# Transformer encoder block in float32 on one core: fixed queue places for the tile and pair operations of the mixed MLP part, spread norm rows, other banks in the last half

## The chip, the cores and the metric

The kernel runs on one core of a Trainium2 chip. The metric is device time in microseconds of one execution, the median of several. Five engines work on their own instruction queues: TensorE (PE, whose weight loads are shown as PEld), VectorE (DVE), ScalarE (ACT), GpSimd (POOL) and SyncE (SP), which here issues the loads and stores. [...]

## What is computed

One layer on 256 tokens of width 2048, all in float32:

```python
x <- LN1(alpha*x + W_out [GQA-group(x) ; MLA-group(x)])   # combined input projection
x <- LN2(alpha*x + CrossAttn(x, LNm(mem)))                # 4 heads, 256 memory tokens
x <- LN3(alpha*x + W2 relu(W1 x)^2)                       # squared-ReLU MLP, width 8192

def squared_relu_mlp(h, w_mlp_in, w_mlp_out):
    return jnp.square(jax.nn.relu(h @ w_mlp_in)) @ w_mlp_out
```

The change lies in the last line, the MLP, which takes the last 60% of the time.

## The kernel before

**Splits.** A float32 product is made of three matmuls on numbers of a shorter format. Each weight piece `raw` (128x1024 float32) is split in two: ACT writes `w_hi` (line 955), then DVE writes `lo = raw - w_hi` (line 956). There are four buffers for `w_hi` and four for `lo`, so a split can be made at most four splits ahead of the matmuls that use it. `mm3` (lines 164 to 166) issues the three matmuls hi*hi, lo*hi, hi*lo. In the list of items below the splits of a pass can be counted 1, 2, 3 and so on; the change counts in them.

**Items.** The hidden layer of the MLP has 64 tiles of 128 columns (4 chunks `c` of `CH` = 16). The first eight are made by `hidden_group`, in two groups of four. After that the order of work is a list `items` of two kinds, and a loop `one_pass(c, q)` goes through it in eight passes (four chunks, two halves `q` of the output columns):

- A hidden tile `("g", c, j)` (`hidden_tile`): two splits, 16 matmuls with `w_hi` (line 1020) and 16 with `lo` (line 1028) into one bank of PSUM `ps`.
- A unit `("u", c, q, p)` multiplies two hidden tiles with their rows of W2. The first six units of a pass (`SEVEN`) use a scheme of seven products in place of eight: 4 splits, of which the last two take sums of weights `s_t`, which DVE makes in three additions (line 948). Units 6 and 7 are plain, with two splits. The last pass has plain units alone.

In passes with q = 1 the list reads g u g u and so on: g has splits 1 and 2, u has 3 to 6, g has 7 and 8, u 9 to 12. In passes with q = 0 it is the same but for one place where two hidden tiles follow each other. Seven passes hold hidden tiles.

**Tile and pair operations.** When a hidden tile is done, `evacuate` brings it out of PSUM: ACT copies one half (line 870) and DVE adds the other (line 871), into one half of a `tmp` tile `h`. When the second of a pair (odd `j`) is there, `stages` follows: `square` is relu and square on ACT (lines 883, 884); `halve` splits the result into `ht`, on ACT (line 874) and DVE (line 875); `add` makes four sums of it on DVE (lines 894, 897, 898); `halve_sums` splits these into `aux` (lines 874, 875 again).

**Pass ends.** After the sixth unit `banks` gets eight additions on DVE that bring the products out of PSUM into `res` (lines 1092, 1094, 1097); at the end of a pass four `merge` calls bring the sums x22, x12, x11, x21 out. `norm_ops(1)` are four multiplications and additions of 128x1024 with the rows of LN2 (line 1194); they must precede the merges of the pass (0, 1).

**What sets the order.** A scheduler places instructions. `queue(ins)` binds an instruction behind the last one queued on its engine, so queued ones keep the order of the code; an instruction under `free_order` is placed by the scheduler. Before, the splits and matmuls are queued, and so are sums and norm rows, which hang at splits through `side`, `banks` and `sums`. The evacuations, most of `stages` (called later, through `late_finish`) and the merges are free.

**Loads.** SP loads each item's 1 MB (line 935) into one of four buffers in turn, and from the item `JOIN` on into one of five: `row_b`, which held the norm rows, joins them.

Of the kernel before, what the change touches and what calls it, by code (L numbers as in the profile page):

```python
# [33 lines left out]
CH = 16  # L34
# [4 lines left out]
def encoder_kernel(ctx: ExitStack, tc: tile.TileContext, t, out):  # L39
# [869 lines left out]
    for c, q in PASSES:  # L909
# [3 lines left out]
        for u in us:  # L913
            n = 2 if q == 0 and u[3] == (CH // 2 - 2 if c else 0) else 1
            items += gs[:n] + [u]
            gs = gs[n:]
    JOIN = items.index(("u", 1, 0, 0))

    def fetch():

# [37 lines left out]
    def part(src, hi=None, lo=None):  # L958
        w = src.shape[1]
        if hi is None:  # L960
            hi = wsp.tile([P, 1024], F32R, tag="w_hi", name="w_hi")
        if lo is None:
            lo = lo_tile()
        queued_split(hi[:, :w], lo[:, :w], src)
        if banks:
            pump()
        if sums:
            sums.popleft()()
        else:
            pump()  # L970
        return hi[:, :w], lo[:, :w]
# [35 lines left out]
    def both(*todo):  # L1007
        return [lambda: [x() for x in todo]]

    now, late_finish = [], []  # L1010

    def hidden_tile(it, ps):

        _, c, j = it
        for h_ in range(2):
            hi, lo = part(raw_of[it][:, h_ * 1024:(h_ + 1) * 1024])
            k0 = 8 * h_

            def w_hi(k):
                queue(nc.tensor.matmul(ps, hi[:, k * P:(k + 1) * P], x2t[:, k0 + k, :],  # L1020
                                       start=k0 + k == 0, stop=k0 + k == KT - 1))

            for k in range(7):
                w_hi(k)
            if h_ == 0:
                w_hi(7)
            for k in range(8):
                queue(nc.tensor.matmul(ps[:, 0:S], lo[:, k * P:(k + 1) * P], x2t[:, k0 + k, 0:S],  # L1028
                                       start=False, stop=False))
            if h_ == 1:  # L1030
                w_hi(7)
        if j % 2 == 0:
            now[:] = [tmp_tile()]
        evacuate(ps, now[0], j % 2)
        if j % 2:
            def rest(h=now[0]):
                for stage in stages(h, c, j // 2, queue if j == CH - 1 else free_order):
                    stage()
            if (c, j) == (0, LEAD + 1):
                x1, x2, x3, x4 = stages(now[0], c, j // 2, queue)  # L1040
                side.extend([x1] + both(x3, x2) + [x4])
            else:
                late_finish.append(rest)

    bank = []
    at = [0]

    def step():

        it = items[at[0]]  # L1050
        at[0] += 1
        if it[0] == "g" and late_finish:
            late_finish.pop()()
        fetch()
        if at[0] < len(items) and not is_seven(it) and is_seven(items[at[0]]):
            push_sums(items[at[0]])
        return it
# [9 lines left out]
    def one_pass(c, q):  # L1067
# [2 lines left out]
        final = (c, q) == PASSES[-1]  # L1070
        if final:
            wide = big.tile([P, 8192], F32R, tag="big", name="wide")
        (x11, x12, x21, x22), (p1, p5, p6, p7) = xs, pt = bank[:4], bank[4:]
        left = {id(ps): len(sevens) * (ps is not x22) + 2 * (len(order) - len(sevens)) for ps in xs}
        left.update({id(ps): len(sevens) for ps in pt})
        left[id(x22)] -= 2 * HELD * final
# [12 lines left out]
        def merge(r, x, op=ALU.add):  # L1089
            if any(r is y for y in fresh):  # L1090
                fresh[:] = [y for y in fresh if y is not r]
                nc.vector.scalar_tensor_tensor(out=r, in0=r, scalar=ALPHA, in1=x, op0=ALU.mult, op1=op)
            else:
                nc.vector.tensor_tensor(out=r, in0=r, in1=x, op=op)  # L1094

        def more(ps, op=ALU.add):
            nc.vector.tensor_tensor(out=m_t, in0=m_t, in1=ps, op=op)
# [2 lines left out]
        while n_unit < len(order):  # L1100
            it = step()
            if it[0] == "g":
                if n_unit == 0:
                    ps = {LEAD: x22, LEAD + 1: x21}[it[2]] if it[1] == 0 else p6
                elif n_seven < len(sevens):
                    ps = x22
                else:
                    spare = spare or [p1, p6]
                    ps = spare[0]
                    spare.reverse()  # L1110
                hidden_tile(it, ps)
                continue
            p, raw, k = it[3], raw_of[it], 2 * it[3]
            n_unit += 1
            if p in sevens:
                if n_seven == 0:
                    while banks:
                        banks.popleft()()
                while sums:
                    sums.popleft()()  # L1120
                for src, todo in ((raw[:, 512:1536], ((p1, a(c, k, 0)), (x12, sm(c, p, 3)))),
                                  (raw[:, 1536:2048], ((x11, a(c, k + 1, 0)),)),
                                  (s_t[:, 0:1024], ((p5, sm(c, p, 1)), (p7, sm(c, p, 0)))),
                                  (s_t[:, 1024:2048], ((p6, sm(c, p, 2)), (x21, a(c, k + 1, 1))))):
                    for (hi, lo), (ps, x) in zip(halves(part(src)), todo):
                        mm(ps, x, hi, lo)
                n_seven += 1
                if at[0] < len(items) and is_seven(items[at[0]]):
                    push_sums(items[at[0]])
                if n_seven == len(sevens):  # L1130
                    nc.scalar.activation(m_t, p1, AF.Copy)

                    rows0, rows1 = late_rows[(c, q)] if (c, q) in late_rows else ([], [])
                    banks.extend(rows0 + [lambda: merge(r11, m_t), lambda: more(p6),
                                  lambda: merge(r12, m_t, ALU.subtract), lambda: more(p7, ALU.subtract)] + rows1 + [
                                  lambda: merge(r21, m_t), lambda: merge(r22, m_t, ALU.subtract),
                                  lambda: merge(r22, p5), lambda: merge(r12, p5)])
            elif final and len(order) - n_unit < HELD:
                n = len(parts) // 2
                for i in range(2):  # L1140
                    o = (2 * n + i) * 1024
                    lo = sums_h[2 * n + i - 1] if n + i else lo_tile()
                    w = halves(part(raw[:, i * 1024:(i + 1) * 1024], wide[:, o:o + 1024], lo))
                    parts.append((k + i, w))
                    for (hi, lo), ps in zip(w, (x12, x11)):
                        mm(ps, a(c, k + i, 0), hi, lo)
            else:
                for i in range(2):
                    w = halves(part(raw[:, i * 1024:(i + 1) * 1024]))
                    for (hi, lo), to in zip(w, ((x12, x22), (x11, x21))):  # L1150
                        for b in range(2):
                            mm(to[b], a(c, k + i, b), hi, lo)
            if q == 1:
                give("h", c, p)
                if p in SEVEN:
                    give("s", c, p)
            if late_finish:
                late_finish.pop()()
        if not final:
            for r, ps in ((r22, x22), (r12, x12), (r11, x11), (r21, x21)):  # L1160
                merge(r, ps)
            if c == NCH - 1:
                banks.extend([lambda b=b, r=r: stats(sts[b], r)
                              for b, r in ((0, r11), (0, r12), (1, r21), (1, r22))])
            return
        pump(len(banks))
        merge(r22, x22)

        def done(b, r, ps):
# [28 lines left out]
    for g in range(LEAD // G):  # L1198
        empty, (first, second) = hidden_group((lambda k: w_mi0[k // 2]) if g == 0 else (lambda k: s_in.next()),
                     att_tile if g % 2 else acc_tile, 0, g * G, first_pair if g == 0 else None)  # L1200
        wait = [lambda: None]

        if g == 0:
            norm_rows(0)
            rows = norm_ops(0)
            (a1, a2, a3, a4), (b1, b2, b3, b4) = first, second
            side.extend(wait * 4 + empty + [a1, b1, a3, a2, a4, b3] + both(b2, rows[0])
                        + both(b4, rows[1]) + rows[2:])
            s_in.split, s_in.beside = queued_split, 2
        else:  # L1210
            (a1, a2, a3, a4), (b1, b2, b3, b4) = first, second
            assert not side
            side.extend(wait + both(*empty) + [a1] + both(a3, a2) + [a4, b1] + both(b3, b2) + [b4])
            norm_rows(1)
    bank[:] = [acc_tile() for _ in range(4)] + [att_tile() for _ in range(4)]
    n1 = norm_ops(1)
    late_rows = {(0, 1): (n1[0::2], n1[1::2])}
    for cq in PASSES:
        one_pass(*cq)

    g3, b3 = s_t, raw_of[items[-5]]
# [137 lines left out]
```

## Time and profile before

| what | value |
| --- | --- |
| runs, us | 1104.68, 1105.43, 1540.56; median 1105.43 |
| profiled execution, us | 1104.5 (span 1102.7, 1.8 us lie around it) |
| mean granted TensorE clock | 0.995 |
| PE busy in the span | 1080.1 us, 98% |
| DVE busy | 936.3 us, 85% |
| ACT busy | 638.4 us, 58% |
| DMA engines, mean share | about 55% |

The profile gives one execution on the chip. A matmul's shown length is longer than the distance to the next one, since matmuls overlap: those of 512 columns are shown with 389 ns and start 227 ns apart. So PE counts as busy through short waits, and a wait is best read from the distance of two starts. DVE and ACT instructions overlap by some 80 ns as well: what one costs in a row of its kind is the distance of starts, 1.135 us for a split of 1024 columns shown with 1.22 us.

The mixed part of the MLP (hidden tiles and units) runs from 447 us to 1046 us. One hidden tile and one unit of seven products there take PE 10.3 us.

### The profile page before, as it was taken

The page shows a single profiled execution, that of the slowest core. Times are in us where ns is not written, and L with a number is a line of the kernel's source. Part 1 is how long each engine was busy: PE and PEld are TensorE (multiplying, and loading weights), DVE is VectorE, ACT ScalarE, POOL GpSimd, SP SyncE. Part 2 cuts the span into 40 slices and gives each one's busy share as a digit, 9 for nine tenths or more (in the row PEclk, how much of TensorE's full clock was granted, in tenths as well). Part 3 has the DMA queues.
Part 4 walks back from the last instruction along what each step waited for, and adds up shares of the span by engine and source line. Part 5 has one row for each costly group of instructions (what it writes and reads, how often), then busy time and mean ns, then how long its engine had stood idle before and what let it go on. Part 6 is the DMA issues. An engine that isn't in the chain of part 4 may idle for free.

```text
span 1102.7 us, 15271 instructions
## 1 busy us (share of the span) xinstructions
PE 1080.1 (98%) x5864; PEld 931.2 (84%) x5864; DVE 936.3 (85%) x1299; ACT 638.4 (58%) x925; POOL 38.2 (3%) x45
## 2 busy tenths in 40 slices
PE   9999999999999999999999899999999999999996
PEld 6988899988999878878888788888888888888885
DVE  6878677678879677999999999899999899999876
ACT  6555566556576426566566466466566566666640
POOL 1502000000100000000000000000000000000000
PEclk9999999999999999999999999999999999999998
DMA  9664453466477445555555546556555555645632
GB/s 329 235 229 139 151 194 136 165 234 232 178 221 259 143 133 191 196 187 202 195 214 196 224 159 223 196 185 229 191 191 214 206 192 195 224 175 194 255 140 77
DMA packets 37369, 215.87 MB, mean 196 GB/s; under 512 B 4272, under 2 KB 5168, under 8 KB 13616
## 3 DMA queue, kind: packets, MB, share of 16 engines
q1 hardware_dynamic: 37296, 214.89, 54.8%
q8 instruction: 46, 0.75, 0.3%
q14 instruction: 27, 0.22, 0.1%
HBM read 212.78 MB, written 2.10 MB: 195 GB/s over the span
## 4 chain that ended last, share of the span: by engine, by line
PE 92%; DVE 4%; DMA 2%; ACT 1%; issue 0%; SPq 0%; POOL 0%; DVEq 0%; ACTq 0%
PE acc L164 13%; PE acc L165 12%; PE acc L166 12%; PE acc L1020 12%; PE acc L1028 6%; PE att L1020 6%; PE att L165 4%; PE att L166 4%; PE att L164 4%; PE att L1028 3%; PE acc L206 2%; PE acc L204 2%; PE acc L205 2%; DVE lo L956 1%; PE acc L213 1%; PE att L213 1%
## 5 line engine op out<-in xcount | busy, mean ns | idle before, releaser
L87 ACT ACTIVATE w_hi<-raw 128x1024 fp32r<-128x1024 f32 (+2 forms) x134 | 131.6, 989 | 115.3 <-PE acc L166 73.1
L88 DVE TENSOR_TENSOR w_lo<-raw,w_hi 128x1024 fp32r<-128x1024 f32 (+2 forms) x130 | 146.1, 1133 | 60.1 <-ACT w_hi L87 59.0
L956 DVE TENSOR_TENSOR lo<-raw,w_hi 128x1024 fp32r<-128x1024 f32 (+1 forms) x156 | 172.9, 1127 | 10.7 <-ACT w_hi L955 10.5
L955 ACT ACTIVATE w_hi<-raw 128x1024 fp32r<-128x1024 f32 (+1 forms) x156 | 148.8, 980 | 30.0 <-PE acc L166 24.4
L1020 PE MATMUL acc<-x2t,w_hi 128*128 128x512 f32 x592 | 153.4, 391 | 0.0
L1020 PEld LDWEIGHTS acc<-x2t,w_hi 128*128 128x128 f32 x592 | 108.9, 189 | 19.7
L956 DVE TENSOR_TENSOR lo<-s_t,w_hi 128x1024 fp32r<-128x1024 f32 x84 | 102.6, 1221 | 12.1 <-ACT w_hi L955 12.1
L955 ACT ACTIVATE w_hi<-s_t 128x1024 fp32r<-128x1024 f32 x84 | 88.8, 1057 | 35.0 <-PE acc L1020 14.0
L1028 PEld LDWEIGHTS acc<-x2t,lo 128*128 128x128 f32 x592 | 80.8, 190 | 5.8
L165 PE MATMUL acc<-lo,ht 128*128 128x512 f32 x213 | 83.0, 390 | 1.1 <-DVE lo L956 1.1
L1028 PE MATMUL acc<-x2t,lo 128*128 128x256 f32 x592 | 82.5, 282 | 0.0
L164 PE MATMUL acc<-w_hi,ht 128*128 128x512 f32 x210 | 82.0, 391 | 0.2 <-DVE res L1094 0.2
L166 PE MATMUL acc<-w_hi,ht 128*128 128x512 f32 x210 | 81.8, 390 | 0.0
L1020 PE MATMUL att<-x2t,w_hi 128*128 128x512 f32 x304 | 78.4, 391 | 0.0
L870 ACT ACTIVATE tmp<-acc 128x256 f32<-128x256 f32 x41 | 15.4, 385 | 101.9 <-PE acc L1020 97.6
L165 PE MATMUL acc<-w_lo,xt 128*128 128x512 f32 (+2 forms) x192 | 69.3, 362 | 0.4 <-DVE w_lo L88 0.4
L166 PE MATMUL acc<-w_hi,xt 128*128 128x512 f32 (+2 forms) x192 | 69.1, 361 | 0.0
L164 PE MATMUL acc<-w_hi,xt 128*128 128x512 f32 (+2 forms) x192 | 66.2, 364 | 0.7 <-ACT w_hi L87 0.7
L1020 PEld LDWEIGHTS att<-x2t,w_hi 128*128 128x128 f32 x304 | 55.8, 189 | 10.0
L956 DVE TENSOR_TENSOR lo<-raw_x,w_hi 128x1024 fp32r<-128x1024 f32 (+1 forms) x50 | 55.3, 1123 | 0.9 <-ACT w_hi L955 0.9
L165 PE MATMUL att<-lo,aux 128*128 128x512 f32 x131 | 51.7, 394 | 2.2 <-DVE lo L956 2.1
L166 PE MATMUL acc<-w_hi,ot 128*128 128x512 f32 (+1 forms) x136 | 51.9, 382 | 0.0
(293 smaller groups left out, 2499.8 us busy)
## 6 DMA issues: line engine op xcount, KB each, us to landing
raw<-in_w_mo SPq DMA_DIRECT2D x41, 1024.0 KB, 4.9
raw<-in_w_mc SPq DMA_DIRECT2D x35, 1024.0 KB, 4.8
raw<-in_w_out SPq DMA_DIRECT2D x16, 1024.0 KB, 4.9
raw_x<-in_w_mc SPq DMA_DIRECT2D x14, 1024.0 KB, 4.8
raw_x<-in_w_mo SPq DMA_DIRECT2D x12, 1024.0 KB, 4.8
row_b<-in_w_mo SPq DMA_DIRECT2D x11, 1024.0 KB, 4.8
raw<-in_w_mi SPq DMA_DIRECT2D x8, 1024.0 KB, 4.9
row_b<-in_w_mc SPq DMA_DIRECT2D x7, 1024.0 KB, 4.8
```

The source lines that it names most:

```text
L87: pin(nc.scalar.activation(hi, src, AF.Copy), pinned)
L88: return pin(nc.vector.tensor_tensor(out=lo, in0=src, in1=f(hi), op=ALU.subtract), pinned)
L164: keep(nc.tensor.matmul(ps, ah, bh, start=start, stop=False))
L165: keep(nc.tensor.matmul(ps, ah, bl, start=False, stop=False))
L166: keep(nc.tensor.matmul(ps, al, bh, start=False, stop=stop))
L204: nc.tensor.matmul(ps, hi, xt[:, k, 0:S], start=k == 0, stop=False)
L205: nc.tensor.matmul(ps, hi, xt[:, k, S:2 * S], start=False, stop=False)
L206: nc.tensor.matmul(ps, lo, xt[:, k, 0:S], start=False, stop=k == nk - 1)
L955: queue(nc.scalar.activation(hi, src, AF.Copy))
L956: queue(nc.vector.tensor_tensor(out=lo, in0=src, in1=f(hi), op=ALU.subtract))
L1020: queue(nc.tensor.matmul(ps, hi[:, k * P:(k + 1) * P], x2t[:, k0 + k, :], start=k0 + k == 0, stop=k0 + k == KT - 1))
L1028: queue(nc.tensor.matmul(ps[:, 0:S], lo[:, k * P:(k + 1) * P], x2t[:, k0 + k, 0:S], start=False, stop=False))
```

## The change

Every tile and pair operation gets a fixed place. A counter rises with each split in `part`; `after(n, todo)` puts an operation into the queues behind the n-th split from now. An evacuation stands three splits behind its tile, `square` directly behind the evacuation of the odd tile, `add` and `halve` one split later, `halve_sums` two splits later. All are queued, and `late_finish` is gone. The merges at a pass end stand behind the third split of the next pass, in another order. The four norm rows, until now pumped with `banks` behind the sixth unit of the pass (0, 1), stand at splits 8, 14, 20 and 26 of that pass. Before the last pass the two sets of four PSUM banks (`xs` and `pt`) change places. `row_b` joins the load buffers one pass earlier.

```diff
-    JOIN = items.index(("u", 1, 0, 0))
+    JOIN = items.index(("u", 0, 1, 7))
...
         queued_split(hi[:, :w], lo[:, :w], src)
+        count[0] += 1
+        while later and later[0][0] <= count[0]:
+            later.pop(0)[1]()
         if banks:
             pump()
...
+    def after(n, *todo):
+
+        later.extend([(count[0] + n, x) for x in todo])
+        later.sort(key=lambda x: x[0])
...
-        evacuate(ps, now[0], j % 2)
+        h = now[0]
+        after(3, lambda: evacuate(ps, h, j % 2, queue))
         if j % 2:
-            def rest(h=now[0]):
-                for stage in stages(h, c, j // 2, queue if j == CH - 1 else free_order):
-                    stage()
-            if (c, j) == (0, LEAD + 1):
-                x1, x2, x3, x4 = stages(now[0], c, j // 2, queue)
-                side.extend([x1] + both(x3, x2) + [x4])
-            else:
-                late_finish.append(rest)
+            square, halve, *sum_up = stages(h, c, j // 2, queue)
+            n = 8 if (c, j) == (0, LEAD + 1) else 3
+            after(n, square)
+            after(n + (j < CH - 1), *sum_up[:1], halve)
+            after(n + 2, *sum_up[1:])
...
-                    rows0, rows1 = late_rows[(c, q)] if (c, q) in late_rows else ([], [])
-                    banks.extend(rows0 + [lambda: merge(r11, m_t), lambda: more(p6),
-                                  lambda: merge(r12, m_t, ALU.subtract), lambda: more(p7, ALU.subtract)] + rows1 + [
+                    banks.extend([lambda: merge(r11, m_t), lambda: more(p6),
+                                  lambda: merge(r12, m_t, ALU.subtract), lambda: more(p7, ALU.subtract),
...
         if not final:
-            for r, ps in ((r22, x22), (r12, x12), (r11, x11), (r21, x21)):
-                merge(r, ps)
+            after(3, *[lambda r=r, ps=ps: queue(merge(r, ps)) for r, ps in ((r12, x12), (r11, x11), (r21, x21), (r22, x22))])
             if c == NCH - 1:
-                banks.extend([lambda b=b, r=r: stats(sts[b], r)
-                              for b, r in ((0, r11), (0, r12), (1, r21), (1, r22))])
+                xs[:], pt[:] = pt[:], xs[:]
+                after(4, *[lambda b=b, r=r: stats(sts[b], r) for b, r in ((0, r11), (0, r12), (1, r21), (1, r22))])
...
-            side.extend(wait + both(*empty) + [a1] + both(a3, a2) + [a4, b1] + both(b3, b2) + [b4])
+            after(2, *empty)
+            for n, x in ((5, a1), (6, a3), (6, a2), (7, a4), (8, b1), (9, b3), (9, b2), (11, b4)):
+                after(n, x)
...
+        if cq == (0, 1):
+            for i, x in enumerate(norm_ops(1)):
+                after(6 * i + 8, x)
```

Where a pair is finished, on ACT. The place is the second unit of the pass (1, 0), whose hidden tile has just ended; `tmp_6183` is the pair's tile, `s_t` holds the unit's weight sums, `raw_4601` the next hidden tile's weights. Before:

```order
L955 ACTIVATE w_hi_6281<-s_t_4191 128x1024
L870 ACTIVATE tmp_6183<-acc_4610 128x256
L955 ACTIVATE w_hi_6290<-s_t_4191 128x1024
L955 ACTIVATE w_hi_6310<-raw_4601 128x1024
L955 ACTIVATE w_hi_6330<-raw_4601 128x1024
L883 ACTIVATE tmp_6183<-tmp_6183 128x512
L955 ACTIVATE w_hi_6355<-raw_4615 128x1024
L884 ACTIVATE tmp_6183<-tmp_6183 128x512
L955 ACTIVATE w_hi_6364<-raw_4615 128x512
L874 ACTIVATE ht_4184<-tmp_6183 128x2x256
```

After the change, at the same place:

```order
L955 ACTIVATE w_hi_6279<-s_t_4191 128x1024
L870 ACTIVATE tmp_6183<-acc_4610 128x256
L883 ACTIVATE tmp_6183<-tmp_6183 128x512
L884 ACTIVATE tmp_6183<-tmp_6183 128x512
L955 ACTIVATE w_hi_6292<-s_t_4191 128x1024
L874 ACTIVATE ht_4184<-tmp_6183 128x2x256
L955 ACTIVATE w_hi_6308<-raw_4601 128x1024
L874 ACTIVATE aux_4185<-tmp_6295 128x512
L955 ACTIVATE w_hi_6330<-raw_4601 128x1024
```

Relu and square (883, 884) stood behind three more splits; now they stand directly behind the evacuation, ahead of the unit's last split.

The same place on DVE. Before:

```order
L956 TENSOR_TENSOR lo2_4188<-s_t_4191,w_hi_6281 128x1024
L871 TENSOR_TENSOR tmp_6183<-acc_4610,tmp_6183 128x256
L956 TENSOR_TENSOR lo3_4189<-s_t_4191,w_hi_6290 128x1024
L956 TENSOR_TENSOR lo0_4186<-raw_4601,w_hi_6310 128x1024
L948 TENSOR_TENSOR s_t_4191<-raw_4615 128x1024
L956 TENSOR_TENSOR lo1_4187<-raw_4601,w_hi_6330 128x1024
L894 TENSOR_TENSOR tmp_6303<-tmp_6183 128x256
L948 TENSOR_TENSOR s_t_4191<-s_t_4191,raw_4615 128x512
L875 TENSOR_TENSOR ht_4184<-tmp_6183,ht_4184 128x2x256
L897 TENSOR_TENSOR tmp_6303<-tmp_6303,tmp_6183 128x128
```

After:

```order
L956 TENSOR_TENSOR lo2_4188<-s_t_4191,w_hi_6279 128x1024
L871 TENSOR_TENSOR tmp_6183<-acc_4610,tmp_6183 128x256
L956 TENSOR_TENSOR lo3_4189<-s_t_4191,w_hi_6292 128x1024
L894 TENSOR_TENSOR tmp_6295<-tmp_6183 128x256
L897 TENSOR_TENSOR tmp_6295<-tmp_6295,tmp_6183 128x128
L898 TENSOR_TENSOR tmp_6295<-tmp_6183,tmp_6295 128x128
L875 TENSOR_TENSOR ht_4184<-tmp_6183,ht_4184 128x2x256
L956 TENSOR_TENSOR lo0_4186<-raw_4601,w_hi_6308 128x1024
L875 TENSOR_TENSOR aux_4185<-tmp_6295,aux_4185 128x512
L948 TENSOR_TENSOR s_t_4191<-raw_4615 128x1024
```

The evacuation (871) keeps its place behind the same split; the pair's additions and halvings now follow one split later, one behind the other, where they were spread over the following items.

The norm rows (1194) on DVE in the pass (0, 1). Before, where the sixth unit has ended:

```order
L956 TENSOR_TENSOR lo0_4186<-raw_x_4192,w_hi_5804 128x1024
L1194 TENSOR_TENSOR res0_1490<-res0_1490,row_b_4193 128x1024 x2
L956 TENSOR_TENSOR lo1_4187<-raw_x_4192,w_hi_5825 128x1024
L956 TENSOR_TENSOR lo2_4188<-raw_4599,w_hi_5850 128x1024
L894 TENSOR_TENSOR tmp_5797<-tmp_5676 128x256
L956 TENSOR_TENSOR lo3_4189<-raw_4599,w_hi_5867 128x1024
L1092 SCALAR_TENSOR_TENSOR res0_1490<-res0_1490,m_t_4190 128x512
L1194 TENSOR_TENSOR res1_1491<-res1_1491,row_b_4193 128x1024
```

After, the first of the four, beside the second hidden tile of the pass:

```order
L956 TENSOR_TENSOR lo2_4188<-raw_4601,w_hi_5381 128x1024
L948 TENSOR_TENSOR s_t_4191<-raw_4615 128x1024
L956 TENSOR_TENSOR lo3_4189<-raw_4601,w_hi_5401 128x1024
L1194 TENSOR_TENSOR res0_1490<-res0_1490,row_b_4193 128x1024
L948 TENSOR_TENSOR s_t_4191<-s_t_4191,raw_4615 128x512 x2
L956 TENSOR_TENSOR lo0_4186<-raw_4615,w_hi_5424 128x1024
```

They moved from the end of the pass, beside plain units, to its first five units, of seven products.

More of the change, by code (lines that the diff above doesn't have):

```diff
@@ L1008, in both @@
         return [lambda: [x() for x in todo]]
-    now, late_finish = [], []
+    now, later, count = [], [], [0]
+    def after(n, *todo):
+        later.extend([(count[0] + n, x) for x in todo])
+        later.sort(key=lambda x: x[0])
     def hidden_tile(it, ps):
@@ L1033, in hidden_tile @@
             now[:] = [tmp_tile()]
-        evacuate(ps, now[0], j % 2)
+        h = now[0]
+        after(3, lambda: evacuate(ps, h, j % 2, queue))
         if j % 2:
-            def rest(h=now[0]):
-                for stage in stages(h, c, j // 2, queue if j == CH - 1 else free_order):
-                    stage()
-            if (c, j) == (0, LEAD + 1):
-                x1, x2, x3, x4 = stages(now[0], c, j // 2, queue)
-                side.extend([x1] + both(x3, x2) + [x4])
-            else:
-                late_finish.append(rest)
-    bank = []
+            square, halve, *sum_up = stages(h, c, j // 2, queue)
[3 more added lines that the diff above has]
+            after(n + 2, *sum_up[1:])
     at = [0]
@@ L1051, in step @@
         at[0] += 1
-        if it[0] == "g" and late_finish:
-            late_finish.pop()()
         fetch()
@@ L1072, in one_pass @@
             wide = big.tile([P, 8192], F32R, tag="big", name="wide")
-        (x11, x12, x21, x22), (p1, p5, p6, p7) = xs, pt = bank[:4], bank[4:]
+        (x11, x12, x21, x22), (p1, p5, p6, p7) = xs, pt
         left = {id(ps): len(sevens) * (ps is not x22) + 2 * (len(order) - len(sevens)) for ps in xs}
@@ L1091, in merge @@
                 fresh[:] = [y for y in fresh if y is not r]
-                nc.vector.scalar_tensor_tensor(out=r, in0=r, scalar=ALPHA, in1=x, op0=ALU.mult, op1=op)
-            else:
-                nc.vector.tensor_tensor(out=r, in0=r, in1=x, op=op)
+                return nc.vector.scalar_tensor_tensor(out=r, in0=r, scalar=ALPHA, in1=x, op0=ALU.mult, op1=op)
+            return nc.vector.tensor_tensor(out=r, in0=r, in1=x, op=op)
         def more(ps, op=ALU.add):
@@ L1156, in one_pass @@
                     give("s", c, p)
-            if late_finish:
-                late_finish.pop()()
         if not final:
-            for r, ps in ((r22, x22), (r12, x12), (r11, x11), (r21, x21)):
-                merge(r, ps)
+            after(3, *[lambda r=r, ps=ps: queue(merge(r, ps)) for r, ps in ((r12, x12), (r11, x11), (r21, x21), (r22, x22))])
             if c == NCH - 1:
-                banks.extend([lambda b=b, r=r: stats(sts[b], r)
-                              for b, r in ((0, r11), (0, r12), (1, r21), (1, r22))])
+                xs[:], pt[:] = pt[:], xs[:]
+                after(4, *[lambda b=b, r=r: stats(sts[b], r) for b, r in ((0, r11), (0, r12), (1, r21), (1, r22))])
             return
         pump(len(banks))
+        assert not later
         merge(r22, x22)
@@ L1212, in encoder_kernel @@
             assert not side
-            side.extend(wait + both(*empty) + [a1] + both(a3, a2) + [a4, b1] + both(b3, b2) + [b4])
+            after(2, *empty)
+            for n, x in ((5, a1), (6, a3), (6, a2), (7, a4), (8, b1), (9, b3), (9, b2), (11, b4)):
+                after(n, x)
             norm_rows(1)
-    bank[:] = [acc_tile() for _ in range(4)] + [att_tile() for _ in range(4)]
-    n1 = norm_ops(1)
-    late_rows = {(0, 1): (n1[0::2], n1[1::2])}
+    xs, pt = [acc_tile() for _ in range(4)], [att_tile() for _ in range(4)]
     for cq in PASSES:
+        if cq == (0, 1):
+            for i, x in enumerate(norm_ops(1)):
+                after(6 * i + 8, x)
         one_pass(*cq)
```

## The prediction

> **What bounds the kernel now.** I read the page first, then stretches of time, then who waits. The page's first part:
>
> ```profile
> span 1102.7 us, 15271 instructions
> PE 1080.1 (98%) x5864; PEld 931.2 (84%) x5864; DVE 936.3 (85%) x1299; ACT 638.4 (58%) x925; POOL 38.2 (3%) x45
> ```
>
> PE bounds the whole. Stretches show where not (start and end, length, then busy us of PE, PEld, DVE, ACT, POOL with counts, granted clock, DMA share, GB/s):
>
> ```profile
> 445.00:490.00 45.00, 41.58 (x209) 33.28 (x208) 40.70 (x56) 29.69 (x44) 0.00 (x0) 1.00 0.57 201
> 490.00:628.00 138.00, 137.61 (x703) 117.36 (x701) 132.44 (x165) 84.14 (x109) 0.00 (x0) 1.00 0.59 211
> 628.00:636.00 8.00, 4.87 (x15) 3.89 (x16) 6.07 (x9) 3.33 (x5) 0.00 (x0) 0.79 0.10 40
> 636.00:1045.00 409.00, 409.00 (x2093) 350.06 (x2092) 379.84 (x473) 256.28 (x333) 0.00 (x0) 1.00 0.56 202
> ...
> 645.42:686.48 41.06, 41.06 (x212) 35.19 (x211) 40.17 (x50) 27.25 (x36) 0.00 (x0) 1.00 0.55 196
> ```
>
> In the mixed part PE waits at the opening (445 to 490) and at 628 to 636, and in the 409 us behind that not at all. The last row holds two pairs (four tiles, four units of seven products): DVE is busy for 40.17 of 41.06 us. So DVE has 0.44 us to spare per pair of 20.7 us. On this number the forecast rests.
>
> What PE waits for, and starts of its tiles' first matmuls (us from the start, length, line, what, count):
>
> ```profile
> PE acc L164 <- DVE res L1094: 3.8, 2, 3.5
> ...
> PEld att L165 <- DVE lo L956: 5.1, 7, 1.3
> ...
> 452.57 2.23 PE L1020 MATMUL acc<-x2t,w_hi 128*128 128x512 f32 x9
> ...
> 464.74 1.98 PE L1020 MATMUL acc<-x2t,w_hi 128*128 128x512 f32 x8
> ...
> 499.89 1.98 PE L1020 MATMUL acc<-x2t,w_hi 128*128 128x512 f32 x8
> ...
> 647.17 1.98 PE L1020 MATMUL acc<-x2t,w_hi 128*128 128x512 f32 x8
> ...
> 657.51 1.98 PE L1020 MATMUL acc<-x2t,w_hi 128*128 128x512 f32 x8
> ...
> 631.13 0.79 PE L164 MATMUL acc<-w_hi,aux 128*128 128x512 f32 x1 [3.52 <-DVE res L1094]
> 631.72 0.63 PE L165 MATMUL acc<-lo,aux 128*128 128x512 f32 x1
> 632.14 0.63 PE L166 MATMUL acc<-w_hi,aux 128*128 128x512 f32 x1
> ...
> 1048.35 0.39 PE L166 MATMUL acc<-w_hi,ht 128*128 128x512 f32 x1
> 1048.97 0.50 PE L164 MATMUL acc<-w_hi,ht 128*128 128x512 f32 x1 [0.24 <-DVE res L1094]
> 1049.31 0.39 PE L165 MATMUL acc<-lo,ht 128*128 128x512 f32 x1
> ```
>
> **What the change can remove.** One tile and one unit take 10.34 us undisturbed (647.17 to 657.51). From 464.74 to 499.89 stand three of them: 35.15 us instead of 31.02. Of the nine matmuls at 452.57 the first ends the tile before, so the next tile starts at 452.80; 464.74 is 11.94 behind that, 1.6 too many: 5.7 us at the opening. At 631 PE waits 3.5 us for a merge that DVE reaches late, since the four norm rows stand before it, and the next eight matmuls start 0.42 apart instead of 0.227 (clock 0.79 in that row of the stretches): 1.6 more, with the first one 5.2 in all. A wait for a merge in the last pass is 0.5 (1048.35 to 1049.31, 0.96 instead of 0.45). Sum 11.4 us: all that can be won, 1.0%, since the prologue, the tail and every matmul stay.
>
> The norm rows leave the pass end, the merges keep the head of the next pass, and the other banks of the last half are empty by then: I count the 5.2 and the 0.5 as gone. `row_b` as a fifth buffer one pass earlier costs nothing: its load is issued behind split 36, the last norm row read it at split 26, and SP has no later load waiting there.
>
> **What the change adds: a wait of DVE at every pair.** Relu and square (883, 884) now stand in ACT's queue ahead of the next `w_hi`, and they need the sum that DVE makes in 871. DVE's next instruction behind 871 is the `lo` of just that `w_hi`, and behind it in DVE's queue is everything else. So the chain 871, 883, 884, 955, 956 runs from engine to engine while DVE has nothing to do. Its links in rows of before:
>
> ```profile
> 542.81 0.38 ACT L870 ACTIVATE tmp<-att 128x256 f32<-128x256 f32 x1 [2.64 <-PE att L1020]
> 543.09 1.05 ACT L955 ACTIVATE w_hi<-s_t 128x1024 fp32r<-128x1024 f32 x1
> 543.23 0.42 DVE L871 TENSOR_TENSOR tmp<-att,tmp 128x256 f32<-128x256 f32 x1 [0.70 <-ACT tmp L870]
> 544.18 1.23 DVE L956 TENSOR_TENSOR lo<-s_t,w_hi 128x1024 fp32r<-128x1024 f32 x1 [0.52 <-ACT w_hi L955]
> ...
> 526.90 0.42 DVE L871 TENSOR_TENSOR tmp<-att,tmp 128x256 f32<-128x256 f32 x1
> 527.35 0.63 ACT L883 ACTIVATE tmp<-tmp 128x512 f32<-128x512 f32 x1 [0.62 <-DVE tmp L871]
> 528.01 0.63 ACT L884 ACTIVATE tmp<-tmp 128x512 f32<-128x512 f32 x1
> ...
> 462.12 0.63 ACT L884 ACTIVATE tmp<-tmp 128x512 f32<-128x512 f32 x1
> 462.65 1.99 ACT L955 ACTIVATE w_hi<-raw 128x1024 fp32r<-128x1024 f32 x2
> ```
>
> By starts: 871 to 883 0.45, 883 to 884 0.66, 884 to 955 0.53, 955 to 956 1.09: 2.73 us. 871 itself takes some 0.34 of DVE, so DVE stands idle for 2.39 us, five times what it has to spare. Before, ACT had three more splits in between, and the row at 544.18 shows what then is left: 0.52.
>
> Could the lead of the splits hide it? A place where DVE is well ahead, the one shown in the section on the change:
>
> ```profile
> 662.85 0.40 PE L1020 MATMUL acc<-x2t,w_hi 128*128 128x512 f32 x1
> ...
> 666.50 0.39 PE L164 MATMUL att<-w_hi,aux 128*128 128x512 f32 x1
> 666.73 0.39 PE L165 MATMUL att<-lo,aux 128*128 128x512 f32 x1
> ...
> 663.28 0.38 ACT L870 ACTIVATE tmp<-acc 128x256 f32<-128x256 f32 x1 [2.64 <-PE acc L1020]
> ```
>
> The tile ends on PE at 663.25 (662.85 and 0.40), and the three splits that may be ready by then feed PE until 666.50; the `lo` of the fourth is needed at 666.73. With the change: 870 at 663.28, 871 at 663.70 (0.42 behind, as at 542.81), `lo` starts 2.73 later at 666.43 and is there 1.22 later, at 667.65. PE waits 0.9 us even with all the lead that four buffers allow. That is the least each pair costs.
>
> Behind it DVE has no lead left, and each further pair costs what DVE lacks: 2.39, plus 0.25 because the pair's additions now follow one another and wait for each other, less the 0.44 to spare: 2.2 us. The rows for the 0.25:
>
> ```profile
> 433.74 0.42 DVE L894 TENSOR_TENSOR tmp<-tmp 128x256 f32<-128x256 f32 x1
> 434.20 0.29 DVE L897 TENSOR_TENSOR tmp<-tmp 128x128 f32<-128x128 f32 x1
> 434.52 0.29 DVE L898 TENSOR_TENSOR tmp<-tmp 128x128 f32<-128x128 f32 x1
> 434.73 0.69 DVE L875 TENSOR_TENSOR ht<-tmp,ht 128x512 fp32r<-128x512 f32 x1
> ...
> 443.81 2.36 DVE L1194 TENSOR_TENSOR res<-res,row_b 128x1024 f32<-128x1024 f32 x2
> 446.08 2.36 DVE L956 TENSOR_TENSOR lo<-raw_x,w_hi 128x1024 fp32r<-128x1024 f32 x2
> ...
> 453.76 1.41 DVE L948 TENSOR_TENSOR s_t<-s_t,raw 128x512 f32<-128x512 f32 x2
> ```
>
> From 894 to 875 it is 0.99 us here, against some 0.74 when they stand between others (each length less the 0.08 of overlap). Bounds: 0 and 0.25; I take 0.25, the order being this one.
>
> Three pairs per pass lie among units of seven products: 0.9 + 2.2 + 2.2 = 5.3 us. The fourth lies at plain units, which ask DVE for two splits and no sums of weights and give it its lead back; I count nothing there. The merges at the third split of a pass find that lead: nothing.
>
> **The sum.** Five passes at 5.3: 26.5. The pass (0, 1): 5.3, and the norm rows, 1.135 us each (443.81, two in 2.36 with 0.08 of overlap), now where DVE lacks time: the first lies half in the lead, 0.6 + 3 x 1.135 = 4.0 (bounds 0 and 4.5; near the upper, since the pairs have used the spare time up). The pass (0, 0): DVE also carries the second group's four evacuations and two pairs. From its first split (446.08) to the end of the fourteenth it has twelve splits of 1.135 and two of 0.6, weight sums for two units (1.135 and 1.32 each), seven evacuations of 0.34, two and a half pairs of operations (2.2 each, the half 1.6), and a wait of 0.8 for a `w_hi` behind relu and square: 28.9 us, so 475.0. PE, had it not waited, would start its third tile at 463.14 and need that split 9.2 later, at 472.3: 2.7 us of the opening's 5.7 stay. Then two pairs, 1.7 and 2.2, and 1.1 in the last unit of seven products: 7.7 (bounds 2 and 11). Together 43.5 us added, 11.4 removed, 32 more. Against the profiled execution's 1104.5 (span 1102.7 and 1.8 around it; the median of the runs is 0.9 higher): 1136.5, I say 1136.
>
> **The rivals.** *It does what a fixed order is for, and the new wait is hidden:* 1104.5 - 11.4 = 1093 us, 1.0% less. For it: every wait of PE in the mixed part is on a late DVE. Against: the `lo` would have to come 0.9 us earlier even in the best place. It decides if the chain from 870 to the end of `lo` stays under 3.45 us; my rows make it 4.37. *Only the least is paid:* DVE regains its lead between pairs; 20 pairs at 0.9, norm rows 2, opening 2.7, less 11.4: 1116. For it: DVE's idle time in stretches is partly waiting for free buffers, so it might have more to spare than I count. Against: 40.17 of 41.06 us is busy time. *The clock falls at the new waits:* at 631 it did, for eight matmuls, 1.6 us. At twenty pairs that is 32 more, 1168. Against: the waits of up to 1.3 us at the opening (the row of PEld) left it at 1.00 (first stretch), and no new one should exceed 2.
>
> [...]
>
> **How the numbers follow.** The full shortage 0.74; the least only 0.13; hidden 0.08; the clock 0.05. The forecast's own range is 1125 (no 0.25, norm rows 2, opening as before) to 1150 (no spare time, all of the norm rows, opening 11). The range reaches down to the second rival: 1115 to 1150, and leaves out 0.13. A measurement tells 2% from no change, 22 us: over 1127.5 lies nearly all of the forecast (0.70 of 0.74) and the clock's case, 0.75; under 1083 nothing that I can name, 0.01; between 0.24.
>
> **What would show it.** In the changed profile DVE at the split behind each odd tile's evacuation should show idle time of about 2.4 us ended by ACT's `w_hi`, twenty times in all, where before it was 0.5; PE should show waits for `lo` of 1 to 2 us in all seven passes with hidden tiles, and DVE's busy share among units of seven products should fall below 0.92. The 3.5 us at 631 and the clock's dip should be gone. I am wrong if PE's starts of tiles stay 10.34 us apart there, or if the idle time ahead of those splits is under 1 us.

## The result, and the profile after

The changed kernel takes 1143.43 us (median of six runs) against 1105.43 before: the ratio is 1.0346, with a 95% interval of 1.0331 to 1.0361. It is slower, by 38 us; the forecast was 1136 us with a range of 1115 to 1150. One run of each kernel was far slower (1540.56 and 1602.80 us) and is left out of the ratio.

The page of the changed kernel, its first part and its chain of work that ended last, and below them the same chain before:

```profile
span 1141.5 us, 15246 instructions
...
PE 1093.6 (96%) x5864; PEld 926.9 (81%) x5864; DVE 940.1 (82%) x1299; ACT 648.3 (57%) x925; POOL 38.3 (3%) x45
...
PE 71%; DVE 18%; ACT 5%; issue 2%; DMA 2%; SPq 0%; POOL 0%; DVEq 0%; ACTq 0%
...
PE 92%; DVE 4%; DMA 2%; ACT 1%; issue 0%; SPq 0%; POOL 0%; DVEq 0%; ACTq 0%
```

PE, DVE and ACT have as many instructions as before, and DVE is busy for 940 us against 936, but the chain now goes through DVE and ACT for 23% of the span instead of 5%. The stretches of the mixed part (columns as in the prediction):

```profile
540.00:628.00 88.00, 81.35 (x399) 66.54 (x399) 77.29 (x95) 49.59 (x61) 0.00 (x0) 0.98 0.52 186
628.00:640.00 12.00, 12.00 (x65) 10.31 (x64) 9.41 (x15) 6.38 (x10) 0.00 (x0) 1.00 0.45 165
640.00:1045.00 405.00, 386.52 (x1920) 318.02 (x1919) 354.31 (x440) 243.79 (x308) 0.00 (x0) 1.00 0.52 185
```

The 3.5 us at 631 are gone. But PE, which did not wait at all behind 636 before, is without work for 18.5 us of 405 by busy time alone, and DVE, which sets its pace, is busy for only 0.87 of the time. Who waits for whom (sum, times, longest, over the whole span; the last line is from the kernel before):

```profile
DVE lo L956 <- ACT w_hi L955: 54.9, 36, 2.3
...
PEld att L165 <- DVE lo L956: 44.6, 42, 2.4
...
PE att L165 <- DVE lo L956: 29.6, 35, 1.9
...
DVE lo L956 <- ACT w_hi L955: 23.7, 45, 2.1
```

DVE waits for ACT's `w_hi`, and PE for DVE's `lo`: the first was 23.7 us in all before, and is 54.9 now. One pair on DVE, then on ACT:

```profile
672.66 1.22 DVE L956 TENSOR_TENSOR lo<-s_t,w_hi 128x1024 fp32r<-128x1024 f32 x1
674.01 0.42 DVE L871 TENSOR_TENSOR tmp<-acc,tmp 128x256 f32<-128x256 f32 x1
676.75 1.23 DVE L956 TENSOR_TENSOR lo<-s_t,w_hi 128x1024 fp32r<-128x1024 f32 x1 [2.32 <-ACT w_hi L955]
677.90 0.42 DVE L894 TENSOR_TENSOR tmp<-tmp 128x256 f32<-128x256 f32 x1
678.35 0.29 DVE L897 TENSOR_TENSOR tmp<-tmp 128x128 f32<-128x128 f32 x1
678.67 0.29 DVE L898 TENSOR_TENSOR tmp<-tmp 128x128 f32<-128x128 f32 x1
678.88 0.68 DVE L875 TENSOR_TENSOR ht<-tmp,ht 128x512 fp32r<-128x512 f32 x1
```

```profile
674.47 0.63 ACT L883 ACTIVATE tmp<-tmp 128x512 f32<-128x512 f32 x1 [0.49 <-DVE tmp L871]
675.14 0.63 ACT L884 ACTIVATE tmp<-tmp 128x512 f32<-128x512 f32 x1
675.67 1.05 ACT L955 ACTIVATE w_hi<-s_t 128x1024 fp32r<-128x1024 f32 x1
```

From the start of 871 to that of `lo` it is 2.74 us, through 883, 884 and 955, and DVE does nothing for 2.32 of them: 894, whose input 884 has ready at 675.77 (675.14 and 0.63), starts at 677.90, behind that `lo`, as it stands in the queue. What PE makes of one pair (the starts of the tiles' first matmuls, and its waits for `lo` between them):

```profile
644.82 1.98 PE L1029 MATMUL acc<-x2t,w_hi 128*128 128x512 f32 x8
...
655.06 0.50 PE L165 MATMUL att<-lo,aux 128*128 128x512 f32 x1 [0.76 <-DVE lo L956]
656.32 1.99 PE L1029 MATMUL acc<-x2t,w_hi 128*128 128x512 f32 x8
...
663.12 0.50 PE L165 MATMUL att<-lo,ht 128*128 128x512 f32 x1 [0.78 <-DVE lo L956]
...
667.83 1.98 PE L1029 MATMUL acc<-x2t,w_hi 128*128 128x512 f32 x8
```

Two tiles and their units take 23.01 us instead of 20.69 (two times 10.34 and rounding), and each pair makes PE wait twice: once right behind the chain, and once more a tile later.

Both kernels have 5864 matmul records in the same order of work, so the start of the same matmul, counted, tells where the time came from. The difference after less before, by stretches of the time before:

| stretch before, us | predicted | measured |
| --- | --- | --- |
| up to 447 (nothing changed there) | 0 | +0.9 |
| 447 to 540, pass (0, 0) with the opening | +7.7 - 5.7 = +2.0 | +1.2 |
| 540 to 637, pass (0, 1) and its end | +9.3 - 5.2 = +4.1 | +5.9 |
| 637 to 1046, five passes | +26.5 | +31.7 |
| 1046 to 1060, last pass | -0.5 | -0.6 |
| sum | +32.1 | +39.0 |

### The profile page after: what moved, and what is told of

The parts are those of the page before. It is cut to its first block, busy times and chain, and to the rows that moved or that the text cites. A ratio compares the mean times of both kernels' runs of the same rounds, so it can differ in the third digit from the quotient of the medians.

```text
span 1141.5 us, 15246 instructions
## 1 busy us (share of the span) xinstructions
PE 1093.6 (96%) x5864; PEld 926.9 (81%) x5864; DVE 940.1 (82%) x1299; ACT 648.3 (57%) x925; POOL 38.3 (3%) x45
## 4 chain that ended last, share of the span: by engine, by line
PE 71%; DVE 18%; ACT 5%; issue 2%; DMA 2%; SPq 0%; POOL 0%; DVEq 0%; ACTq 0%
PE acc L165 10%; PE acc L164 10%; PE acc L166 10%; DVE lo L956 9%; PE acc L1029 6%; PE att L1029 5%; PE att L165 4%; PE att L166 3%; DVE s_t L948 3%; PE acc L1037 3%; PE att L164 3%; PE att L1037 3%; ACT w_hi L955 2%; PE acc L206 2%; PE acc L204 2%
## 5 line engine op out<-in xcount | busy, mean ns | idle before, releaser
L165 PE MATMUL att<-lo,aux 128*128 128x512 f32 x139 | 57.7, 415 | 17.4 <-DVE lo L956 17.4
L165 PE MATMUL acc<-lo,ht 128*128 128x512 f32 (+1 forms) x188 | 73.6, 392 | 0.0
L164 PE MATMUL acc<-w_hi,ht 128*128 128x512 f32 x186 | 72.8, 392 | 0.0
L166 PE MATMUL acc<-w_hi,ht 128*128 128x512 f32 x186 | 72.8, 391 | 0.0
L164 PE MATMUL att<-w_hi,aux 128*128 128x512 f32 x139 | 56.4, 406 | 1.2 <-ACT w_hi L955 0.7
```

Source lines behind the costliest of these rows:

```text
L164: keep(nc.tensor.matmul(ps, ah, bh, start=start, stop=False))
L165: keep(nc.tensor.matmul(ps, ah, bl, start=False, stop=False))
L166: keep(nc.tensor.matmul(ps, al, bh, start=False, stop=stop))
```

## The experiments

Ten kernels, each also timed against the kernel before on the same chip. `n` is the split at which relu and square stand, counted from the odd tile's end.

**Relu and square three splits later (sq6).** An edit of one line in the changed kernel:

```diff
-            n = 8 if (c, j) == (0, LEAD + 1) else 3
+            n = 8 if (c, j) == (0, LEAD + 1) else 3 if j == CH - 1 else 6
```

> The changed kernel with relu and square of a pair three splits later than the odd tile's evacuation (split 6 instead of 3), and with them the pair's additions; all else as changed. My theory: the loss is DVE's wait behind 871 for the w_hi that stands behind relu and square. With three more w_hi ahead of them on ACT it goes: the group L956 waiting for ACT's w_hi L955 falls from 54.9 us to about 25 (before: 23.7), PE's waits for lo from 74 us to under 20, the time to 1095-1104. Rival A, the pair's additions that follow one another on DVE are the cause: they still follow one another here, so the time stays near 1143. Rival B, the merges, the banks or the norm rows cost the time: over 1130.

Measured: 1102.24 us, 0.9972 of before (0.9962 to 0.9981). The wait of DVE for `w_hi` falls to 21.1 us. So the place of relu and square, with the pair's additions behind them, makes the loss (the next runs part the two), and without it the change is worth 0.3%. Not all of the time comes back: two tiles still take 20.94 us.

```profile
643.00 1.98 PE L1029 MATMUL acc<-x2t,w_hi 128*128 128x512 f32 x8
...
663.94 1.98 PE L1029 MATMUL acc<-x2t,w_hi 128*128 128x512 f32 x8
```

**One split later (sq4).** The same with 4 in place of 6.

> The same, one split later instead of three (split 4 instead of 3). My theory: one w_hi (1.05 us) then stands between 870 and relu, so that DVE has one lo (1.22 us) to do while ACT squares; DVE's idle time per pair falls from 2.4 to about 1.2 us, PE's least cost of the first pair of a pass from 1.0 to nothing, and further pairs cost about 1.0: between the two, 1103-1118. Rival, the additions in one chain or the merges: unchanged, near 1143.

Measured: 1126.35 us, 1.0183 (1.0164 to 1.0202); slower than either number I gave. On DVE:

```profile
668.93 0.42 DVE L871 TENSOR_TENSOR tmp<-acc,tmp 128x256 f32<-128x256 f32 x1
669.88 1.23 DVE L956 TENSOR_TENSOR lo<-s_t,w_hi 128x1024 fp32r<-128x1024 f32 x1 [0.53 <-ACT w_hi L955]
672.01 1.23 DVE L956 TENSOR_TENSOR lo<-raw,w_hi 128x1024 fp32r<-128x1024 f32 x1 [0.90 <-ACT w_hi L955]
```

The `w_hi` in between doesn't take the wait away, it splits it: 0.53 for the first, 0.90 for the second, 1.43 where I had 1.2. And I had let the first pair of a pass go free, which it doesn't: its two tiles take 22.14 us (640.61 to 662.75), as those of the others do.

**The fixed places alone (pairs_alone).** The kernel before, with the counter and `after`, and nothing else:

```diff
-        evacuate(ps, now[0], j % 2)
+        h = now[0]
+        after(3, lambda: evacuate(ps, h, j % 2, queue))
         if j % 2:
...
+            square, halve, *sum_up = stages(h, c, j // 2, queue)
+            n = 8 if (c, j) == (0, LEAD + 1) else 3
+            after(n, square)
+            after(n + (j < CH - 1), *sum_up[:1], halve)
+            after(n + 2, *sum_up[1:])
```

> The kernel before with nothing but the fixed places of the tile and pair operations (evacuation at split 3, relu and square at split 3 of the odd tile); norm rows, merges, banks and JOIN as before. My theory: nearly the whole loss is here: 1137-1147, with the 3.5 us wait for the merge at the pass's end still there. Rival B, the merges, banks or norm rows: under 1115.

Measured: 1142.48 us, 1.0331 (1.0314 to 1.0349), within 1 us of the whole change. The merges, banks, norm rows and `JOIN` together neither win nor lose beside it. The 3.5 us for a merge that I expected to stay are not there, though: the longest wait at that pass's end is 1.7 by starts. What took them away there is not shown.

**The additions late, relu and square not (late_rest).**

```diff
-            after(n + (j < CH - 1), *sum_up[:1], halve)
-            after(n + 2, *sum_up[1:])
+            after(n + 5 * (j < CH - 1), *sum_up[:1])
+            after(n + 6 * (j < CH - 1), halve)
+            after(n + 7, *sum_up[1:])
```

> The changed kernel with relu and square where the change has them (split 3), but the pair's additions spread over splits 8 to 10 instead of 4 and 5. My theory, in which the additions' chain is worth 0.25 us a pair at most: 1136-1145, DVE still idle for 2.3 us behind each odd tile's 871. Rival A, the additions in one chain are the cause: near 1100.

Measured: 1141.56 us, 1.0324 (1.0308 to 1.0339). DVE still stands idle for 2.31 us behind 871. Where the additions stand hardly matters as long as the chain is there.

**Relu at split 3, square at split 6 (relu_only).**

```diff
-            n = 8 if (c, j) == (0, LEAD + 1) else 3
-            after(n, square)
+            n = 8 if (c, j) == (0, LEAD + 1) else 3 if j == CH - 1 else 6
+            if n == 6:
+                after(3, lambda: queue(nc.scalar.activation(h, h, AF.Relu)))
+                after(n, lambda: queue(nc.scalar.activation(h, h, AF.Square)))
+            else:
+                after(n, square)
```

The additions stand behind square, as in sq6, and the pairs that sq6 leaves in place are left here too.

> The changed kernel with relu at split 3 as the change has it, but square at split 6 and the pair's additions at 7 and 8. My theory: what counts is how long ACT works between 871 and the next w_hi. Half of that work is gone, 0.66 us of 2.39 a pair; three pairs in each of seven passes are 14 us: 1127-1132, DVE idle for about 1.7 us at 20 splits. Rival, it is the place of the additions and halvings that counts, not ACT's work: near 1102, as sq6. Rival, any operation of the pair ahead of that w_hi makes DVE wait a full round: 1138-1143.

Measured: 1123.62 us, 1.0164 (1.0149 to 1.0180).

```profile
668.16 0.41 DVE L871 TENSOR_TENSOR tmp<-acc,tmp 128x256 f32<-128x256 f32 x1
670.22 1.22 DVE L956 TENSOR_TENSOR lo<-s_t,w_hi 128x1024 fp32r<-128x1024 f32 x1 [1.65 <-ACT w_hi L955]
```

The idle time is what I expected (1.65 against 1.7), one of the two ACT operations (0.66) less than with both. Both rivals fall: the wait goes with ACT's work, not with the additions' place and not by whole rounds. The time is 3.4 us under my lower number, because a pair gained 0.89 us and not 0.66 (22.95 to 22.06): DVE's idle time as a whole falls by 0.80, since 871 no longer waits 0.13 for ACT's copy either, and the other 0.09 is in DVE's work.

**Norm rows back to the pass end (norm_back).** The changed kernel with `late_rows`, and `JOIN`, as before.

> The changed kernel with norm rows and JOIN alone back behind the sixth unit. My prediction put the spread rows at 4.0 us in the pass (0, 1), where the pairs have used up DVE's spare time; the trace has two waits of 2.1 us there and one dip of the clock. By that: 1137-1140, the waits in that pass about 1 us each as in the others, and no dip. Rival, the rows only move their cost to the pass end: 1142-1144.

Measured: 1141.77 us, 1.0332 (1.0318 to 1.0346); 1.7 us less than the change by the medians, with intervals that overlap. It lies between my numbers and the rival's. The two long waits in that pass and the clock's dip are gone (the mean granted clock of the profiled execution is 0.997 against 0.995), and two others have come at its plain units:

```profile
611.64 1.22 PE L1037 MATMUL att<-x2t,lo 128*128 128x256 f32 x8 [1.04 <-DVE lo L956]
...
620.08 2.09 PE L1029 MATMUL att<-x2t,w_hi 128*128 128x512 f32 x8 [1.53 <-DVE m_t L1100]
```

**The same with relu and square at split 6 (sq6_normback), and the norm rows in wider places (sq6_rows,** `after(10 * i + 5, x)` **instead of** `6 * i + 8`**).**

> Relu and square at split 6 as in the run sq6, but norm rows and JOIN back where they were before the change (behind the sixth unit of the pass (0, 1)); the merges stay at the third split of the next pass. My prediction had the old wait of 3.5 us go because rows and merges part; if it was the merges at the pass end that made PE wait, it stays away here too, the three waits of 2.5 us in the pass go, and some 1 us comes at the plain units: 1100-1102. If the rows at the pass end alone made it, a wait of about 3 us is back with the clock's dip: 1103-1106.

> Relu and square at split 6 as in the run sq6, and the four norm rows at splits 5, 15, 25 and 35 of the pass (0, 1) instead of 8, 14, 20 and 26. In the run sq6 PE still waited 0.94, 0.57 and 0.94 us in that pass, and DVE stood idle for 1.79 us about split 5. My theory, that the rows cost what DVE lacks between them: the first goes into the idle time, the others have 20 us each to be made up for; 1 to 2.5 us less than sq6, 1100-1101. Rival, the rows don't matter: 1102, as sq6.

Measured: 1101.70 us, 0.9966 (0.9953 to 0.9978), and 1101.79, 0.9968 (0.9958 to 0.9978). By time neither can be told from sq6, so the 1 to 2.5 us that I gave to the wider places do not show. The traces differ: with the rows back, the wait at the pass's end does not return (one of 0.56 us at 631.47 is the longest), so the rows need not move for it. Whether the merges must is open: pairs_alone, with rows and merges both in their old places, lacks that wait too, and no run puts the merges alone back.

**One split for each addition (spread).** In sq6_normback, `add` is cut into its three instructions (894, 897, 898), which no longer stand in a row, and the halvings go one and two splits later:

```diff
+            if n == 6 and sum_up:
+                for i, x in enumerate(sum_up[0].parts):
+                    after(n + 1 + i, x)
+                after(n + 2, halve)
+                after(n + 4, sum_up[1])
+            else:
...
```

> Relu and square at split 6, norm rows as before the change (the run sq6_normback), and the three instructions of the pair's additions (894, 897, 898) one split apart each, the halvings between and behind them. In the run sq6 two tiles and units still took 20.94 us instead of 20.69 before the change. My prediction had put 0.25 us a pair on the additions that wait for one another. If that is right, two tiles take 20.7 again, 20 pairs give 5 us: 1096-1099. Rival, the 0.25 is something else (the evacuation waiting for ACT's copy, or the idle 0.53 behind it): 1101-1103, 20.9 us.

Measured: 1097.59 us, 0.9931 (0.9918 to 0.9944): faster than both kernels. Two tiles take 20.69 us again, as before the change:

```profile
639.90 1.98 PE L1042 MATMUL acc<-x2t,w_hi 128*128 128x512 f32 x8
...
650.24 1.98 PE L1042 MATMUL acc<-x2t,w_hi 128*128 128x512 f32 x8
...
660.59 1.98 PE L1042 MATMUL acc<-x2t,w_hi 128*128 128x512 f32 x8
```

The three additions on DVE, each with what follows it (896, 901 and 904 are the lines 894, 897 and 898 of the others):

```profile
644.16 0.42 DVE L896 TENSOR_TENSOR tmp<-tmp 128x256 f32<-128x256 f32 x1
644.50 0.68 DVE L969 TENSOR_TENSOR lo<-raw_x,w_hi 128x512 fp32r<-128x512 f32 x1
645.10 0.28 DVE L901 TENSOR_TENSOR tmp<-tmp 128x128 f32<-128x128 f32 x1
645.30 0.68 DVE L875 TENSOR_TENSOR ht<-tmp,ht 128x512 fp32r<-128x512 f32 x1
...
647.04 0.28 DVE L904 TENSOR_TENSOR tmp<-tmp 128x128 f32<-128x128 f32 x1
647.24 0.42 DVE L871 TENSOR_TENSOR tmp<-acc,tmp 128x256 f32<-128x256 f32 x1
```

By starts they take 0.34, 0.20 and 0.20 us, 0.74 in all, against 0.98 in a row in the changed kernel (677.90 to 678.88). So the additions in a row cost about 0.25 us a pair, the term of the prediction. The time of two tiles alone would not show it, since PE is the bound here, and the 0.50 us for which DVE stands idle behind 871 in sq6_normback are not there either.

**The first pair of each pass alone at split 3 (first_only).** In sq6:

```diff
-            n = 8 if (c, j) == (0, LEAD + 1) else 3 if j == CH - 1 else 6
+            n = 8 if (c, j) == (0, LEAD + 1) else 3 if j in (1, LEAD + 1, CH - 1) else 6
```

> The run sq6, with relu, square and the additions of each pass's first pair alone back at split 3 where the change has them (six passes); all other pairs stay at split 6. It prices the term of my prediction that now looks too small. As the prediction had it, the first pair finds DVE's lead and costs 0.9 us: 1102.2 + 6 x 0.9 = 1107 to 1108. As the starts of the tiles in the changed kernel have it, it costs nearly as much as the others, 1.9 to 2.2 us, because the pair's additions and halvings follow in the next tile, when the lead is spent: 1113 to 1116.

Measured: 1114.80 us, 1.0085 (1.0070 to 1.0100). Against sq6's 0.9972 that is 12.5 us for six pairs, 2.1 each. The trace has the same two waits as a pair in the changed kernel, the second one a tile behind the first:

```profile
645.53 0.50 PE L165 MATMUL att<-lo,aux 128*128 128x512 f32 x1 [0.76 <-DVE lo L956]
...
653.59 0.50 PE L165 MATMUL att<-lo,ht 128*128 128x512 f32 x1 [0.78 <-DVE lo L956]
```

Beside each other, for two tiles and units behind 639 us (the start of one tile to that of the second next; in after, late_rest and sq4 the second pair of the pass, from 667.83, 667.63 and 662.75), with DVE's idle time there (gaps over 0.05 us between its instructions):

| kernel | us | DVE idle | rest |
| --- | --- | --- | --- |
| before | 20.69 | 0.30 | PE is the bound |
| after | 22.95 | 2.45 | 20.50 |
| late_rest | 22.75 | 2.31 | 20.44 |
| sq4 | 22.11 | 1.54 | 20.57 |
| relu_only | 22.06 | 1.65 | 20.41 |
| sq6 | 20.94 | 0.51 | 20.43 |
| spread | 20.69 | 0 | PE is the bound |

In the five in the middle DVE sets the pace: its work takes 20.4 to 20.6 us, and each microsecond in which it waits for ACT is one on the clock.

## Why the prediction was right, and where it was not

**The new wait** was the mechanism, and its size was right: the chain was forecast at 2.73 us and DVE's idle time at 2.39; the trace has 2.74 and 2.32. Each of its four links was the distance of two starts in rows of before, and none changed by more than 0.01. PE waits for `lo` in all seven passes, and DVE's busy share among units of seven products is 0.89 (20.50 of the 22.95 us in the table) where I had said below 0.92. The idle time stands fourteen times in this form, not twenty: at the third pair of six passes ACT's copy of `m_t` (1134) comes in between and the wait falls in two, 0.49 and 1.44 us by the trace at 697.9 and 700.0.

**A further pair of a pass** was put at 2.2 us; two tiles take 22.95 instead of 20.69, 2.26. Its three numbers hold nearly: the idle time above, with 0.13 ahead of 871, is 2.45; the 0.25 is in the run spread; and for 0.44 to spare sq6 gives 0.51, since with 0.51 idle and 0.25 for the additions it loses 0.25. With these 2.45 + 0.25 - 0.51 = 2.19.

**The first pair of a pass** is the step that failed in size. I put it at 0.9, "even with all the lead that four buffers allow", and took the lead to pay for the rest. The run first_only measured 2.1. The 0.9 is there: PE's first wait is 1.03 by the distance of starts at 655.06. Behind it, though, come the additions and halvings of that same pair, 2.2 us of DVE's work by starts (654.92 to 658.25 without a split), with no lead left; that is the second wait, 0.95 at 663.12. In late_rest, where they stand later, the next tile lacks that wait (656.97 to 667.63, 10.66 us), but the tile before is longer (12.99). The walk stopped one tile too early. With 2.1 a pass comes to 6.5; it measured 6.3 (31.7 for five), where I had 5.3. The five passes so hold 5.2 of the 6.9 us that are missing in the sum.

**The pass (0, 1)** lost 5.9 net instead of 4.1. Up to the matmul at 615 before it lost 10.9, forecast 9.3, of which the first pair explains 1.2. For the norm rows, forecast at 4.0, norm_back gives the price, counted by matmuls as in the table: from 540 up to the matmul at 600 the change loses 10.3 and norm_back 6.0, so rows and the clock's dip cost some 4.4; behind it norm_back loses 2.6 more at its plain units, so that in the whole pass the move costs 1.8. The gain at the pass's end, 5.0, was forecast as 5.2. The number was right and my reason for it, that rows and merges part, is not shown: the wait is gone in sq6_normback without the rows' move, and in pairs_alone without either.

**The opening** kept 2.3 us of waits, in the changed kernel as in sq6 (0.72 and 1.57 by starts, in the changed kernel at 470.63 and 476.03), forecast 2.7 of 5.7; the pass (0, 0) as a whole came out at +1.2 for +2.0. **Merges, banks, `JOIN`** at nothing: in pairs_alone, without them, the five passes lose 31.9 us where the change loses 31.7. The last pass's wait, forecast to go for 0.5, stays there and goes in the change (0.6).

**The rivals.** That the wait is hidden falls with the first view. That only the least is paid was forecast at 1116: DVE regains no lead between pairs that stand so close. The clock did not fall at twenty waits, as the third rival had it, but once, behind a wait of 1.91 us, under the 2 that I had set as a bound. That of two such waits only one is followed by a fall I had not foreseen; the last section has both.

## What to carry to other kernels

When an instruction that waits for engine B's result is put into engine A's queue, look at what B has next: if that is the very thing that A makes behind it, B stands still until A has worked through the round, as DVE did here for 2.32 us at a pair, though over the span it was busy for 82% and ACT for 57%. Leave as many of A's next results ahead of it as B needs to work through the round: here three were enough (0.51 us idle in sq6), and one only split the wait (0.53 and 0.90 us in sq4; two were not tried). When walking through such a place by hand, go on until the work that was put off has been done as well, not only to the first wait.

## What the runs showed of the hardware

The clock fell behind a shorter wait than the 3.52 us of before (at 631.13). In the changed kernel a wait of 1.91 us at 569.36 is followed by half the clock, while one of 1.92 us at 595.08 is not:

```profile
569.36 0.50 PE L165 MATMUL att<-lo,ht 128*128 128x512 f32 x1 [1.91 <-DVE lo L956]
...
595.08 0.50 PE L165 MATMUL att<-lo,ht 128*128 128x512 f32 x1 [1.92 <-DVE lo L956]
```

Three stretches of the changed kernel, ahead of the fall, in it and behind it (the granted clock is third from the end):

```profile
555.00:570.63 15.63, 12.70 (x61) 9.77 (x61) 13.22 (x18) 9.63 (x13) 0.00 (x0) 1.00 0.38 138
570.63:574.05 3.42, 3.42 (x10) 2.68 (x9) 3.42 (x5) 2.12 (x2) 0.00 (x0) 0.50 0.90 307
574.05:1060.00 485.95, 462.97 (x2303) 381.15 (x2302) 426.08 (x529) 288.70 (x365) 0.00 (x0) 1.00 0.53 187
```

The clock is at 0.50 from 570.63 to 574.05. Behind that, up to 1060 us, it is at 1.00, and the second wait lies in this stretch. The fall cost 1.4 us beside the wait (seven matmuls 0.43 apart instead of 0.227). What parted the two waits is not shown.
